# Rotary products and cached-score products of a hybrid decoder step put on VectorE in quarter steps, with half of the largest group's cached scores computed inside attention

## The chip, the cores and the metric

The kernel runs on one core of one Trainium2 chip, in one launch. The metric is the device time of that core in microseconds (us). The kernel before was timed three times: 1585.9, 1585.96 and 1590.62 us, a median of 1585.96 us. The profile is a further execution, with its own time of 1582.48 us.

## What is computed

The reference is one inference step of a two-layer decoder trunk for 512 prompt tokens and 8 x 8 sample tokens (576 tokens in all, 1024 channels). Layer 0 mixes with dilated attention, layer 1 with a state-space layer; each is followed by a gated feed-forward part. The change lies in the attention layer alone:

```python
qkv = (h @ w_qkv).reshape(B, T, 3, N_DIL, N_HEAD_SLOTS, HEAD_DIM)
q = rope(rmsnorm(qkv[:, :, 0], q_gain), pos)      # per head of 64
k = rope(rmsnorm(qkv[:, :, 1], k_gain), pos)
v = qkv[:, :, 2]
...
s = jnp.einsum('bqhd,bqkhd->bqhk', q_blk, kf) * (HEAD_DIM ** -0.5)
...
o = jnp.einsum('bqhk,bqkhd->bqhd', p, vf)         # for each of 3 groups
...
wts = jax.nn.softmax(jnp.stack(lses, axis=0), axis=0)
return jnp.einsum('gbqh,gbqhd->bqhd', wts, jnp.stack(outs, axis=0))
```

There are three groups (g = 0, 1, 2) with window and dilation (128, 1), (512, 4) and (2048, 16), each with 8 heads of 64. A sample token attends to cached keys and values (`cache_kv_w128`, `_w512`, `_w2048`) at those strides and to the 8 new tokens of its sequence. In group 2 the dilation is larger than the 8 new tokens, so each of the 8 queries of a sequence has its own 128 cached keys: 8 sequences x 8 queries x 128 keys x 512 channels are read. `rope` turns each head's two halves: x1*cos - x2*sin and x2*cos + x1*sin.

## The kernel before

**Projections** (`qkv_phase`, about 12 to 345 us of the profile). Nine chunks of 512 output channels are worked off in the order q, k, v of group 2, then of group 1, then of group 0. A chunk (`qkv_chunk`) has four steps of two 128-row weight tiles. In a step a weight block `raw` of 512 KB is loaded, split into a high part `whi` (ScalarE, L95) and a low part `wlo` (VectorE, L96: `raw - whi`), and multiplied with the split activations on TensorE (L320 to L326). `whi` and `wlo` have two buffers, so the split of a block waits for the matmuls of the block two before it, and TensorE waits for the split. Here and below line numbers are those of the kernel before.

After a q or k chunk its five token tiles are read out of PSUM (L476), squared and summed for the norm (L480, L481, then five small VectorE instructions L115 and L105 to L109), and a closure `finish(t)` per tile is put on the list `late`. `finish` rotates: VectorE multiplies with the cosines (L493, `t1`), GpSimd (POOL) multiplies the swapped halves with the sines (L495, `t2`) and adds (L496), VectorE scales with the norm (L498, `o`), TensorE transposes (L502) and ScalarE copies the result to `qT` or `kT`.

After each of the 36 steps a function `step()` runs: it pops `late` as the table `LATE` says, and starts the cached scores that the table `PLAN` names for that step. For groups 0 and 1 that is `score(gi, b)` for a sequence b, which transposes cached keys on TensorE. For group 2 it is `score2(b)`: four times it loads a tile `kc` of cached keys (512 KB) and a tile `qb` with the queries spread to all 128 partitions (512 KB, from the scratch `qscr`), multiplies the two (L404, by turns on VectorE and on POOL, into `kc`), and sums over each head's 64 channels with two reduces on VectorE (L406). The sums of all eight queries are then transposed, joined with the scores against the new keys, masked and stored in `Sall` (L408 to L417). All tiles `kc` and `qb` come from one pool `kst` of six buffers.

**Attention** (`attn_phase`, 345 to 477 us). Eight `decode(b)`, one per sequence, take the softmax of `Sall[b]`, transpose it (L628, L631), spread it into a padded tile (L633, L642), and multiply it with the cached values on TensorE (L655), whose seven tiles per sequence (six of 512 KB, one of 256 KB) come through the same six buffers of `kst`; then the new values (L658), a copy (L660) and a transpose back (L662). Four `prompt_pair(hp)`, one per pair of heads, run the prompt's scores, softmax (L598, L566 to L571 on VectorE, L568 on ScalarE), transposes (L602) and value products (L609, L615) in four rounds r each. The program's order is decode 2hp, pair hp, decode 2hp+1. After it, `wo_phase` needs all of `att`.

**Order.** The framework that builds the program (the tile scheduler) reorders instructions of an engine within what dependences and buffers allow; each engine then works strictly in the order written. DMAs of this part are issued by SyncE (SP), also in order: an issue that waits for a buffer holds up every one behind it.

Of the kernel before, what the change touches and what calls it, by code (L numbers as in the profile page):

```python
# [8 lines left out]
F32 = mybir.dt.float32  # L9
# [22 lines left out]
SCALE = HD ** -0.5  # L32
KST = 6
RV, RF = 0.0, 0.7
LATE = (2, 2, 1, 0)
PLAN = {11: (2,), 12: (2,), 14: (2,), 16: (2,), 20: (2,), 21: (2,), 22: (2, 1), 23: (2, 1), 24: (1,), 25: (1,), 26: (1,), 28: (1,), 30: (1,), 32: (1,), 34: (0, 0, 0), 35: (0, 0, 0)}


def dram(ap, off, dims):
    return bass.AP(tensor=ap.tensor, offset=ap.offset + off, ap=[list(d) for d in dims])  # L40
# [317 lines left out]
    return t  # L358


def qkv_phase(nc, tc, A, es, L):
    v, s, g, te = nc.vector, nc.scalar, nc.gpsimd, nc.tensor
    ident, rsqrt, pool = L["ident"], L["rsqrt"], L["pool"]
# [29 lines left out]
    wk = e3.enter_context(pool("wk1", bufs=2))  # L393
    qscr, vscr = L["qscr"], L["vscr"]

    def score2(b):
        q0 = T + b * 8
        P = dk.tile([128, 4, 4, 8], F32, name="ks")
        g.memset(P, 0.0)
        for c0 in range(0, 8, 2):  # L400
            kc = cache_tile(nc, A, kst, "kc", 2, b, c0, 2, 0)
            qb = kst.tile([128, 2, 512], F32, name="kc")
            nc.sync.dma_start(qb, dram(qscr, (b * 8 + c0) * 512, [[0, 128], [512, 2], [1, 512]]))
            (g if c0 % 4 else v).tensor_tensor(kc, kc, qb, OP.mult)  # L404
            for c in range(2):
                v.tensor_reduce(P[:, :, 0:2, c0 + c], kc[:, c].rearrange("p (a h d) -> p a h d", a=4, h=2), AX.X, OP.add)  # L406
        Q = dk.tile([128, 5, 4, 32], F32, name="Qz")
        g.memset(Q[:, 0], 0.0)  # L408
        for h in range(2):
            hs = slice(h * 64, h * 64 + 64)  # L410
            g.tensor_copy(Q[hs, 0, :, h * 8:h * 8 + 8], qT[2][hs, :, q0:q0 + 8])
        Sd = psd.tile([128, 136], F32, name="Sd")
        te.transpose(Sd[:, 0:128], P.rearrange("p a b c -> p (a b c)"), ident)
        for hp in range(4):
            te.matmul(Sd[hp * 32:hp * 32 + 32, 128:136], Q[:, 0, hp, :], kT[2][:, hp, q0:q0 + 8], start=True, stop=True,
                      tile_position=(0, hp * 32), skip_group_check=True)
        v.tensor_tensor_reduce(Sall[:, b, 2, :], Sd, md[:, 2, :], 1.0, -3e38, OP.add, OP.max, mx3[:, b, 2:3])  # L417

    def score(gi, b):
        q0 = T + b * 8  # L420
# [32 lines left out]
    turn = [0]  # L453

    def step():
        for _ in range(LATE[turn[0] % 4]):
            if late:
                late.pop(0)()
        for gi in PLAN.get(turn[0], ()):
            if fill[gi]:  # L460
                b = fill[gi].pop(0)
                score2(b) if gi == 2 else score(gi, b)
        turn[0] += 1

    late = []

    def qk_chunk(gi, part):
        ps = qkv_chunk(nc, A, L, x, part, gi, step, 0.0, x.prep if gi == 2 and part == 0 else None)
        sh = wk.tile([128, 5, 8], F32, name="sh")
        v.memset(sh[64:128, 4], 1.0)  # L470
        at = []
        for t in range(5):
            pp = 128 if t < 4 else 64
            a = wk.tile([128, 512], F32, name="a", bufs=5)
            if t < 4:
                s.activation(a, ps[t], AF.Copy, scale=(x.rb if gi == 0 else x.rc)[:, t:t + 1])  # L476
# [3 lines left out]
            s.activation(sq[:pp].rearrange("p h d -> p (h d)"), a[:pp], AF.Square)  # L480
            v.tensor_reduce(sh[:pp, t], sq[:pp], AX.X, OP.add)  # L481
            at.append(a)
        rq = wk.tile([128, 5, 8], F32, name="rq")
        rsqrt(rq, sh, 1.0 / HD, wk, [128, 5, 8])

        def finish(t):
            pp = 128 if t < 4 else 64
            ti = 8 if t == 4 else (4 + t if gi == 0 else t)
            a = at[t]
            t1 = wk.tile([128, 8, 64], F32, name="t1")  # L490
            t2 = wk.tile([128, 8, 2, 32], F32, name="t2", bufs=1)
            a4 = a.rearrange("p (h t d) -> p h t d", h=8, t=2)
            v.tensor_tensor(t1[:pp], a[:pp].rearrange("p (h d) -> p h d", h=8), C[part][:pp, ti, None, :].to_broadcast([pp, 8, 64]), OP.mult)  # L493
            Sv = S[part][:, ti, :].rearrange("p (t d) -> p t d", t=2)
            g.tensor_tensor(t2[:pp], a4[:pp, :, ::-1, :], Sv[:pp, None].to_broadcast([pp, 8, 2, 32]), OP.mult)  # L495
            g.tensor_tensor(t1[:pp], t1[:pp], t2[:pp].rearrange("p h t d -> p h (t d)"), OP.add)  # L496
            o = wk.tile([128, 512], F32, name="o")
            v.tensor_tensor(o[:pp].rearrange("p (h d) -> p h d", h=8), t1[:pp], rq[:pp, t, :, None].to_broadcast([pp, 8, 64]), OP.mult)  # L498
            dst = (qT, kT)[part][gi]
            pt = ptp.tile([128, 4, 128], F32, name="pt")  # L500
            for hp in range(4):
                te.transpose(pt[:, hp, :pp], o[:pp, hp * 128:(hp + 1) * 128], ident[:pp, :pp])  # L502
            s.activation(dst[:, :, t * 128:t * 128 + pp], pt[:, :, :pp], AF.Copy)
# [4 lines left out]
            if part == 1 and t == 4:  # L508
                fill[gi] += range(NB)

        late.extend((lambda t=t: finish(t)) for t in range(5))

# [23 lines left out]
    for gi in (2, 1, 0):  # L536
        while fill[gi]:
            score2(fill[gi].pop(0)) if gi == 2 else score(gi, fill[gi].pop(0))
# [10 lines left out]
def attn_phase(nc, tc, A, es, L):  # L549
# [20 lines left out]
        v.reciprocal(rd, den)  # L570
        v.tensor_scalar(sm, sm, rd, None, op0=OP.mult)  # L571

    def prompt_pair(hp):
        O = pO.tile([128, 4, 4, 32], F32, name="O")
        P0 = [wk.tile([128, 2, 4, 4, 32], F32, name=f"P0_{h}", bufs=1) for h in range(2)]
        for r in range(4):
            P12 = {}
            S2 = [pS.tile([128, 512], F32, name="S") for _ in range(2)]
            half = [slice(0, 64), slice(64, 128)]
            for b in range(4):  # L580
                for h in range(2):
                    hs = half[h]
                    q = qT[0][hs, hp, b * 128 + r:b * 128 + 128:4]
                    if b:
                        k = kT[0][hs, hp, (b - 1) * 128:(b + 1) * 128]
                        te.matmul(S2[h][b * 32:b * 32 + 32, 0:256], q, k, start=True, stop=True, tile_position=(h * 64, b * 32))
                    else:
                        k = kT[0][hs, hp, 0:128]
                        te.matmul(S2[h][0:32, 0:256].rearrange("p (a c) -> p a c", a=2), q, k[:, None, :].to_broadcast([64, 2, 128]), start=True, stop=True)
            for gi in (1, 2):  # L590
                sl = slice(r * 128, r * 128 + 128)
                for h in range(2):
                    te.matmul(S2[h][:, (gi + 1) * 128:(gi + 2) * 128], qT[gi][half[h], hp, sl], kT[gi][half[h], hp, sl], start=True, stop=True)
            for h in range(2):
                S = S2[h]
                sm = wk.tile([128, 512], F32, name="sm", bufs=3)
                mx = wk.tile([128, 1], F32, name="mx")
                v.tensor_tensor_reduce(sm, S, mp[:, r, :], 1.0, -3e38, OP.add, OP.max, mx)  # L598
                expnorm(sm, mx)
                pt = pP.tile([128, 4, 128], F32, name="pt")  # L600
                for c in range(4):
                    te.transpose(pt[:, c, :], sm[:, c * 128:(c + 1) * 128], ident)  # L602
                s.activation(P0[h][:, :, :, r, :], pt[:, 0:2, :].rearrange("p a (b i) -> p a b i", b=4), AF.Copy)
                p12 = wk.tile([128, 2, 128], F32, name="P12", bufs=3)
                v.tensor_copy(p12, pt[:, 2:4, :])
                P12[h] = p12
            for gi in (1, 2):
                for h in range(2):
                    te.matmul(O[h * 64:h * 64 + 64, r], vt[gi][:, r, (2 * hp + h) * 64:(2 * hp + h + 1) * 64], P12[h][:, gi - 1, :], start=gi == 1 and r == 0, stop=False, skip_group_check=True)  # L609
# [9 lines left out]
    def decode(b):  # L619
# [44 lines left out]
        for h in range(2):  # L664
            hs = slice(h * 64, h * 64 + 64)
            v.tensor_copy(att[hs, :, q0:q0 + 8], ot[hs, :, h * 8:h * 8 + 8])

    for hp in range(4):
        decode(2 * hp)
        prompt_pair(hp)  # L670
        decode(2 * hp + 1)


# [618 lines left out]
```

## Time and profile before

| | |
|---|---|
| median of three runs | 1585.96 us |
| the profiled execution's own time | 1582.48 us |
| its span, first to last instruction | 1580.7 us |
| TensorE (PE) busy | 1519.8 us, 96% |
| VectorE (DVE) busy | 917.6 us, 58% |
| ScalarE (ACT) busy | 527.0 us, 33% |
| GpSimd (POOL) busy | 433.4 us, 27% |
| mean granted TensorE clock | 0.992 |

The 1.8 us between span and own time lie outside the instructions. Times in the profile are us from the span's start. A row of the groups of instructions reads: line, engine, operation, tile written <- tiles read, shape, count | busy us, mean ns of one | idle time before them and what ended it. A row of the stages reads: start:end, width, then for each engine its busy us and (count), then the granted TensorE clock (1.00 is full), the share in which the 16 DMA engines were busy, and the GB/s they moved. A row of the timeline reads: start, duration, engine, line, operation, names, shape, count and, in brackets, the engine's idle time just before and what ended it. Each value product of a decode (L655) shows as two records, so that its 52 make 104.

### The profile page before, as it was taken

How to read it: one execution, taken by the hardware profiler on the slowest of the kernel's cores; microseconds unless marked ns; L12 is line 12 of the kernel's file. 1: busy time of each engine (PE TensorE's matmuls, PEld its weight loads, DVE VectorE, ACT ScalarE, POOL GpSimd, SP SyncE). 2: the span in 40 equal slices, each digit the busy share in tenths (PEclk: the TensorE clock that was granted, in tenths of full speed). 3: DMA queues.
4: the chain of work that ended last, by engine and by line, in shares of the span. 5: the costliest groups of instructions: out<-in, count | busy, mean ns of one | idle time of the engine just before them, and what ended most of it. 6: DMA issues, size and time to landing. Idle time of an engine off the chain costs nothing. (4 is left out here: it accounts for less than half of the span.)

```text
span 1580.7 us, 28939 instructions
## 1 busy us (share of the span) xinstructions
PE 1519.8 (96%) x12010; PEld 1425.8 (90%) x12010; DVE 917.6 (58%) x1557; ACT 527.0 (33%) x790; POOL 433.4 (27%) x407
## 2 busy tenths in 40 slices
PE   7989899979989999999999999999999999999998
PEld 6979777756669999999999999999999999999998
DVE  4787987445546785378878756775353333333332
ACT  5524334444434322123212244343242212221222
POOL 2464865440002101944524521021011001100100
PEclk9999999999998999999999999999999999999999
DMA  7398796484675555588767774875555555433212
GB/s 226 99 319 306 267 353 225 136 289 159 235 267 161 186 187 193 186 276 309 249 230 239 239 267 149 268 221 191 192 186 187 203 206 211 144 135 102 81 61 80
DMA packets 193843, 324.82 MB, mean 205 GB/s; under 512 B 40112, under 2 KB 137520, under 8 KB 192176
## 3 DMA queue, kind: packets, MB, share of 16 engines
q1 hardware_dynamic: 184256, 304.95, 56.5%
q10 hardware_dynamic: 9456, 18.03, 3.2%
q8 instruction: 94, 1.54, 0.4%
q14 instruction: 37, 0.30, 0.1%
HBM read 290.40 MB, written 119.83 MB: 260 GB/s over the span
## 5 line engine op out<-in xcount | busy, mean ns | idle before, releaser
L96 DVE TENSOR_TENSOR wlo<-raw,whi 128x1024 fp32r<-128x1024 f32 x200 | 256.2, 1282 | 265.1 <-ACT whi L95 261.6
L95 ACT ACTIVATE whi<-raw 128x1024 fp32r<-128x1024 f32 x200 | 208.2, 1042 | 522.3 <-PE acc L102 396.2
L102 PE MATMUL acc<-xgl,whi 128*128 128x288 f32 x1760 | 378.6, 296 | 1.0 <-DVE xgl L168 1.0
L102 PE MATMUL acc<-xgh,wlo 128*128 128x288 f32 x1760 | 377.6, 296 | 0.0
L102 PE MATMUL acc<-xgh,whi 128*128 128x288 f32 x1760 | 377.1, 296 | 0.1
L102 PEld LDWEIGHTS acc<-xgl,whi 128*128 128x128 f32 x1760 | 282.7, 188 | 2.6 <-DVE xgl L168 1.3
L102 PEld LDWEIGHTS acc<-xgh,wlo 128*128 128x128 f32 x1760 | 282.8, 188 | 0.6 <-issue 0.2
L102 PEld LDWEIGHTS acc<-xgh,whi 128*128 128x128 f32 x1760 | 281.7, 188 | 0.5 <-DVE gt L728 0.3
L730 POOL TENSOR_TENSOR gt<-gt,rstd 128x576 f32<-128x576 f32 x44 | 77.2, 1756 | 433.2 <-ACT gt L729 433.1
L102 PE MATMUL acc<-hh,whi 128*128 128x288 f32 x704 | 151.4, 296 | 0.0
L102 PE MATMUL acc<-hh,wlo 128*128 128x288 f32 x704 | 151.3, 295 | 0.0
L102 PE MATMUL acc<-hl,whi 128*128 128x288 f32 x704 | 151.1, 295 | 0.0
L321 PE MATMUL acc<-wlo,xh 128*128 128x512 f32 x288 | 118.7, 414 | 9.6 <-DVE wlo L96 9.6
L320 PE MATMUL acc<-whi,xh 128*128 128x512 f32 x288 | 111.5, 414 | 3.9 <-ACT a L522 3.7
L322 PE MATMUL acc<-whi,xl 128*128 128x512 f32 x288 | 113.7, 403 | 0.0
L102 PEld LDWEIGHTS acc<-hh,wlo 128*128 128x128 f32 x704 | 113.2, 188 | 0.2 <-issue 0.2
L102 PEld LDWEIGHTS acc<-hl,whi 128*128 128x128 f32 x704 | 113.0, 188 | 0.2 <-issue 0.2
L102 PEld LDWEIGHTS acc<-hh,whi 128*128 128x128 f32 x704 | 113.1, 188 | 0.0
L188 POOL TENSOR_TENSOR ssum<-ssum,sq 128x576 f32<-128x576 f32 x21 | 35.5, 1690 | 271.8 <-ACT sq L187 271.8
L321 PEld LDWEIGHTS acc<-wlo,xh 128*128 128x128 f32 x288 | 77.9, 270 | 16.1 <-DVE wlo L96 11.8
L320 PEld LDWEIGHTS acc<-whi,xh 128*128 128x128 f32 x288 | 75.5, 272 | 11.4 <-ACT a L522 4.9
L322 PEld LDWEIGHTS acc<-whi,xl 128*128 128x128 f32 x288 | 77.0, 271 | 4.2
(346 smaller groups left out, 2102.1 us busy)
## 6 DMA issues: line engine op xcount, KB each, us to landing
o_kv_s<-cache_kv_w SPq DMA_DIRECT2D x64, 1020.0 KB
kc<-cache_kv_w SPq DMA_DIRECT2D x96, 512.0 KB
raw<-ffn_w_gate SPq DMA_DIRECT2D x44, 512.0 KB
raw<-ffn_w_up SPq DMA_DIRECT2D x44, 512.0 KB
raw<-ffn_w_down SPq DMA_DIRECT2D x40, 512.0 KB
raw<-w_qkv SPq DMA_DIRECT2D x36, 512.0 KB
kc<-qscr SPq DMA_DIRECT2D x32, 512.0 KB
o_kv_s<-cache_kv_w SPq DMA_DIRECT2D x16, 1008.0 KB
```

What stands on the lines that cost most here:

```text
L95: s.activation(hi, raw, AF.Copy)
L96: v.tensor_tensor(lo, raw, hi.bitcast(F32), OP.subtract)
L102: te.matmul(ps[:, c, :HN], w, x[:, c * HN:(c + 1) * HN], start=first and i == 0, stop=last and i == 2)
L188: g.tensor_tensor(self.ss, self.ss, sq, OP.add)
L320: te.matmul(ps[t], ah, wh[:, k2, :], start=k == 0, stop=False)
L321: te.matmul(ps[t], ah, wl[:, k2, :], start=False, stop=False)
L322: te.matmul(ps[t], al, wh[:, k2, :], start=False, stop=k == KT - 1)
L730: g.tensor_tensor(t, t, nin.r, OP.mult)
```

## The change

Four things change. First, the sine product and the addition of the rotation (L495, L496) go from POOL to VectorE. Second, the products of `score2` are cut into four parts per sequence, each with one product and two reduces, so that the table names a part and not a sequence; in the projections all of them run on VectorE. Third, only the first four sequences (`EARLY = 4`) are done in the projections; the 16 parts of the other four are called in `prompt_pair`, two at the start of each round r, with the product on POOL, so that they stand in the first two pairs. Fourth, `LATE` and `PLAN` have new numbers. Sums over the heads stay on VectorE everywhere. The arithmetic and the work of TensorE are the same in total.

```diff
-LATE = (2, 2, 1, 0)
-PLAN = {11: (2,), 12: (2,), 14: (2,), 16: (2,), 20: (2,), ...
+EARLY = 4
+LATE, LAST = (2, 1, 1, 1), (2, 2, 1, 0)
+PLAN = {9: (2,), 11: (2,), 12: (2,), 13: (2,), 14: (2,), 15: (2,), ...
...
+def products(nc, A, L, eng, P, b, part):
+    kst, c0 = L["kst"], 2 * part
+    kc = cache_tile(nc, A, kst, "kc", 2, b, c0, 2, 0)
+    qb = kst.tile([128, 2, 512], F32, name="kc")
+    nc.sync.dma_start(qb, dram(L["qscr"], (b * 8 + c0) * 512, [[0, 128], [512, 2], [1, 512]]))
+    eng.tensor_tensor(kc, kc, qb, OP.mult)
+    for c in range(2):
+        nc.vector.tensor_reduce(P[:, :, 0:2, c0 + c], kc[:, c].rearrange("p (a h d) -> p a h d", a=4, h=2), AX.X, OP.add)
+
+def close2(nc, L, dk, psp, nm, P, b):
...
+    Sd = psp.tile([128, 136], F32, name=nm)
+    nc.tensor.transpose(Sd[:, 0:128], P.rearrange("p a b c -> p (a b c)"), L["ident"])
+    for hp in range(4):
+        nc.tensor.matmul(Sd[hp * 32:hp * 32 + 32, 128:136], Q[:, hp, :], kT[:, hp, q0:q0 + 8], start=True, stop=True,
+                         tile_position=(0, hp * 32), skip_group_check=True)
+    nc.vector.tensor_tensor_reduce(L["Sall"][:, b, 2, :], Sd, L["md"][:, 2, :], 1.0, -3e38, OP.add, OP.max, L["mx3"][:, b, 2:3])
...
-    def score2(b):
...
-            (g if c0 % 4 else v).tensor_tensor(kc, kc, qb, OP.mult)
...
+    def score2(b, part):
+        if part == 0:
+            prods[b] = dk.tile([128, 4, 4, 8], F32, name="P2", bufs=1)
+            g.memset(prods[b], 0.0)
+        products(nc, A, L, v, prods[b], b, part)
+        if part == 3:
+            close2(nc, L, dk, psd, "Sd", prods.pop(b), b)
...
-            g.tensor_tensor(t2[:pp], a4[:pp, :, ::-1, :], Sv[:pp, None].to_broadcast([pp, 8, 2, 32]), OP.mult)
-            g.tensor_tensor(t1[:pp], t1[:pp], t2[:pp].rearrange("p h t d -> p h (t d)"), OP.add)
+            v.tensor_tensor(t2[:pp], a4[:pp, :, ::-1, :], Sv[:pp, None].to_broadcast([pp, 8, 2, 32]), OP.mult)
+            v.tensor_tensor(t1[:pp], t1[:pp], t2[:pp].rearrange("p h t d -> p h (t d)"), OP.add)
...
-    def prompt_pair(hp):
+    def prompt_pair(hp, fill):
...
         for r in range(4):
+            for _ in range(2):
+                fill()
...
+    rest = [(b, p) for b in range(EARLY, NB) for p in range(4)]
+    def score2():
+        if not rest:
+            return
+        b, part = rest.pop(0)
...
+        products(nc, A, L, g, prods[b], b, part)
+        if part == 3:
+            close2(nc, L, dk, pD, "Sd", prods.pop(b), b)
...
-        prompt_pair(hp)
+        prompt_pair(hp, score2)
```

Below, line numbers are of the kernel in question: in the changed kernel the split is L98, the rotation L507 to L512, the product L368, its reduces L370, the closing L381 to L385, the decode's value product L672 and its transposes L645 and L679.

VectorE in the projections, while the group-2 queries are being rotated (`C` and `S` are the cosine and sine tables, `t` the two products, `rq` the norms). Before, ahead of a split:

```order
L498 TENSOR_TENSOR o<-t_537,rq 128x512
L498 TENSOR_TENSOR o<-t_550,rq 128x512
L493 TENSOR_TENSOR t_597<-a,C_150 128x512
L493 TENSOR_TENSOR t_610<-a,C_150 128x512
L96 TENSOR_TENSOR wlo<-raw,whi 128x1024
```

Now:

```order
L98 TENSOR_TENSOR wlo<-raw,whi 128x1024
L507 TENSOR_TENSOR t_597<-a,C_150 128x512
L507 TENSOR_TENSOR t_644<-a,C_150 128x512
L510 TENSOR_TENSOR t_597<-t_597,t_598 128x512
L509 TENSOR_TENSOR t_645<-a,S_152 128x512
L510 TENSOR_TENSOR t_644<-t_644,t_645 128x512
L512 TENSOR_TENSOR o<-t_597,rq 128x512
L509 TENSOR_TENSOR t_692<-a,S_152 64x512
L512 TENSOR_TENSOR o<-t_644,rq 128x512
L98 TENSOR_TENSOR wlo<-raw,whi 128x1024
```

A tile's rotation is now four VectorE instructions instead of two, so that eight stand between these two splits, and none of them waits for POOL any more.

SyncE's queue at the start of attention. `kc<-cache_kv_w` of 128x512 is the first value tile of a decode, the six of 128x2x512 behind it are its others; before, the tiles of decode 1 follow those of decode 0 directly:

```order
L357 DMA kc<-cache_kv_w 128x512
L357 DMA kc<-cache_kv_w 128x2x512 x6
L357 DMA kc<-cache_kv_w 128x512
L357 DMA kc<-cache_kv_w 128x2x512 x5
L645 DMA vn<-vscr 8x512 x3
```

Now the keys and queries (`kc<-qscr`) of eight parts stand between them:

```order
L359 DMA kc<-cache_kv_w 128x2x512 x7
L367 DMA kc<-qscr 128x1024
L359 DMA kc<-cache_kv_w 128x2x512
L367 DMA kc<-qscr 128x1024
...
L359 DMA kc<-cache_kv_w 128x2x512
L367 DMA kc<-qscr 128x1024
L359 DMA kc<-cache_kv_w 128x512
L359 DMA kc<-cache_kv_w 128x2x512 x6
L359 DMA kc<-cache_kv_w 128x512
```

The seven in the first row are the six of decode 0 and the first part's keys; decode 1 begins at the row of 128x512 after the eighth `qscr`. Decode 2 follows it, then eight more parts, then decode 3.

TensorE at the end of attention, from the last value products of the last pair (L615, now L632) to the first matmul of `wo_phase` (`ath`). Before:

```order
L615 MATMUL O<-P_1_4787,vt_2826 64x4x32
L655 MATMUL Sd<-kc,Pz_3331 32x128 x48
L658 MATMUL Sd<-vn,pn 32x128 x4
L662 MATMUL Sd<-ident,os 128x128
L102 MATMUL acc_5181<-ath,whi 128x288 x2
```

Now:

```order
L632 MATMUL O<-P_1_4787,vt_2513 64x4x32
L672 MATMUL Sd<-kc,Pz_3166 32x128 x8
...
L645 MATMUL Sd<-ident,Sall 128x128 x3
...
L672 MATMUL Sd<-kc,Pz_3167 32x128 x48
...
L672 MATMUL Sd<-kc,Pz_3166 32x128 x48
...
L672 MATMUL Sd<-kc,Pz_3167 32x128 x48
L675 MATMUL Sd<-vn,pn 32x128 x4
L679 MATMUL Sd<-ident,os 128x128
L104 MATMUL acc_5181<-ath,whi 128x288 x2
```

Before, one decode (the eighth) stands behind the last pair. Now the end of the fifth and the whole of the sixth, seventh and eighth stand there, with nothing of a pair between them.

More of the change, by code (lines that the diff above doesn't have):

```diff
@@ L394, in qkv_phase @@
     qscr, vscr = L["qscr"], L["vscr"]
-    def score2(b):
[L397 to L417, printed above, removed]
+    prods = {}
+    def score2(b, part):
[5 more added lines that the diff above has]
+            close2(nc, L, dk, psd, "Sd", prods.pop(b), b)
     def score(gi, b):
@@ L455, in step @@
     def step():
-        for _ in range(LATE[turn[0] % 4]):
+        for _ in range((LATE if turn[0] < 32 else LAST)[turn[0] % 4]):
             if late:
@@ L460, in step @@
             if fill[gi]:
[L461 to L462 removed]
+                x_ = fill[gi].pop(0)
+                score2(*x_) if gi == 2 else score(gi, x_)
         turn[0] += 1
@@ L507, in finish @@
                 nc.sync.dma_start(qscr, o[:64])
-            if part == 1 and t == 4:
-                fill[gi] += range(NB)
+            if t == 4 and part == (gi < 2):
+                fill[gi] += range(NB) if gi < 2 else [(b, p) for b in range(EARLY) for p in range(4)]
         late.extend((lambda t=t: finish(t)) for t in range(5))
@@ L535, in qkv_phase @@
     v_chunk(0, wk, vt)
-    for gi in (2, 1, 0):
+    assert not fill[2]
+    for gi in (1, 0):
         while fill[gi]:
-            score2(fill[gi].pop(0)) if gi == 2 else score(gi, fill[gi].pop(0))
+            score(gi, fill[gi].pop(0))
     e3.close()
```

13 lines of the change are left out of this document (12 added, 1 removed).

## The prediction

> **What bounds the kernel now.** I read the stages first: PE's idle time in each is its width less PE's busy time.
>
> ```profile
> 12.00:320.00 308.00, 289.15 (x1563) 250.53 (x1563) 223.87 (x306) 129.91 (x199) 173.78 (x169) 0.99 0.70 240
> 320.00:345.00 25.00, 17.61 (x288) 13.01 (x294) 10.34 (x37) 13.69 (x26) 13.31 (x30) 1.00 0.79 263
> 345.00:360.00 15.00, 12.49 (x170) 6.99 (x154) 4.85 (x17) 3.38 (x9) 0.00 (x0) 0.77 1.04 381
> 360.00:380.00 20.00, 20.00 (x184) 12.43 (x184) 14.51 (x64) 9.79 (x28) 0.00 (x0) 1.00 0.09 34
> 380.00:468.00 88.00, 83.80 (x1248) 57.24 (x1248) 47.04 (x203) 35.66 (x98) 0.00 (x0) 1.00 0.75 259
> 468.00:477.00 9.00, 4.53 (x102) 3.10 (x92) 0.81 (x3) 2.27 (x4) 0.00 (x0) 0.75 0.47 136
> 477.00:1580.70 1103.70, 1088.74 (x8473) 1079.63 (x8472) 612.36 (x922) 327.08 (x421) 245.75 (x203) 1.00 0.56 191
> ```
>
> PE bounds everything; its work does not change, so only its idle time can. That is 18.9 us in the nine chunks (12 to 320), 7.4 us behind the last chunk, 11.2 us in attention (2.5 + 0 + 4.2 + 4.5). From 477 on nothing moves, and I cost that part at nothing. PE's own waits in the chunks say what can go:
>
> ```profile
> PE acc L321 <- DVE wlo L96: 9.6, 5, 4.8
> PE acc L320 <- ACT a L522: 3.7, 3, 3.0
> PE pt L276 <- ACT xq L271: 2.5, 1, 2.5
> PE pt L502 <- DVE o L498: 1.6, 2, 1.2
> ```
>
> The longest of them, in the timeline of PE, VectorE and POOL:
>
> ```profile
> 97.45 0.82 PE L321 MATMUL acc<-wlo,xh 128*128 128x512 f32 x1 [4.77 <-DVE wlo L96]
> ...
> 93.11 0.96 DVE L106 TENSOR_TENSOR sq<-rq 128x40 f32<-128x40 f32 x1
> 94.00 3.40 DVE L96 TENSOR_TENSOR wlo<-raw,whi 128x1024 fp32r<-128x1024 f32 x1
> ...
> 93.98 2.34 POOL L404 TENSOR_TENSOR kc<-kc 128x1024 f32<-128x1024 f32 x1
> 96.27 2.26 POOL L495 TENSOR_TENSOR t<-a,S 128x512 f32<-128x512 f32 x1
> ...
> 72.57 1.21 DVE L96 TENSOR_TENSOR wlo<-raw,whi 128x1024 fp32r<-128x1024 f32 x1
> ```
>
> And the stage row of the 3.4 us behind that wait, the clock in the third column from its end:
>
> ```profile
> 97.00:100.40 3.40, 2.95 (x7) 2.41 (x8) 3.37 (x3) 0.00 (x0) 3.40 (x2) 0.50 0.55 164
> ```
>
> The same split takes 1.21 us elsewhere and 3.40 us here: it ends about a microsecond after POOL's product. [...] PE pays twice, since its granted clock is 0.50 in the 3.4 us after the stall (1.7 us lost).
>
> **The rotations.** The groups of VectorE and POOL up to 345 us:
>
> ```profile
> L495 POOL TENSOR_TENSOR t<-a,S 128x512 f32<-128x512 f32 (+1 forms) x30 | 53.4, 1779 | 13.6 <-ACT a L476 12.0
> L496 POOL TENSOR_TENSOR t<-t,t 128x512 f32<-128x512 f32 (+1 forms) x30 | 52.7, 1755 | 50.0 <-DVE t L493 36.8 <-ACT t L480 11.5 <-ACT qT L503 0.7
> L404 POOL TENSOR_TENSOR kc<-kc 128x1024 f32<-128x1024 f32 x16 | 41.1, 2570 | 10.2 <-DMA kc<-qscr 9.8
> ...
> L96 DVE TENSOR_TENSOR wlo<-raw,whi 128x1024 fp32r<-128x1024 f32 x38 | 55.0, 1450 | 27.9 <-ACT whi L95 27.7
> L406 DVE TENSOR_REDUCE ks<-kc 128x8 f32<-128x512 f32 x64 | 40.4, 674 | 0.3
> L106 DVE TENSOR_TENSOR sq<-rq 128x40 f32<-128x40 f32 x6 | 7.0, 1171 | 0.2
> ...
> 70.27 0.69 DVE L498 TENSOR_TENSOR o<-t,rq 128x512 f32<-128x512 f32 x1 [1.19 <-POOL t L496]
> ```
>
> POOL loses 106 us. VectorE gains 60 instructions; the nearest row is the free 0.69 us (a reversed operand could make it dearer, POOL's 1.78 us is the far bound): 41 us. It loses 32 of the 64 reduces, 32 x 0.674 = 22 us; its 16 products stay 16. It also loses the waits for POOL: on the splits alone 38 x (1.450 - 1.21) = 9 us, on the small norm step 6 x about 1 us. So VectorE stays near its 224 us of 308, but in pieces that no POOL instruction stretches, and spread: a sequence's scores put 2 x 1.21 + 8 x 0.674 = 7.8 us into one step before (a product has the split's 128x1024 shape), a part puts 1.21 + 2 x 0.674 = 2.6 us, and a step lasts about 8.6 us (308 in 36). Hence wlo's 9.6 us, o's 1.6 us and one clock drop of 1.7 us should go: 12.9, taken as **-13 us**. The ACT waits I leave standing. Bounds: -6 if half the queueing stays, -20 if all of 18.9 - 2.5 and two drops go.
>
> [...]
>
> **The closings.** Four transposes with their small matmuls move from one stage to the other. PE does them either way: nothing, their waits being counted below.
>
> **DMAs in attention.** Sixteen parts, two tiles each, join SP's queue between the decodes' value tiles:
>
> ```profile
> kc<-qscr SPq DMA_DIRECT2D x32, 512.0 KB
> ...
> DMA packets 16856, 30.41 MB, mean 230 GB/s; under 512 B 3200, under 2 KB 3264, under 8 KB 16708
> ...
> xT<-x_scr SPq DMA_DIRECT2D x1, 2304.0 KB
> ```
>
> Decode 0's last products and decode 1's first stand here on PE:
>
> ```profile
> 356.52 0.64 PE L655 MATMUL Sd<-kc,Pz 128*32 128x128 f32 x16
> ...
> 381.62 0.43 PE L655 MATMUL Sd<-kc,pa 128*32 128x128 f32 x8
> ```
>
> That is 16 x 2 x 0.524 = 16.8 MB on top of 30.4 MB (345 to 477), 47 MB. The full rate is that of the stage 345 to 360, 381 GB/s at a share of 1.04: 124 of 132 us. So the engines suffice on average, and the idle 360 to 380 takes 7.6 MB of the first eight parts' 8.4. [...]
>
> In the chunks SP's queue is rid of the same 16.8 MB; PE names no DMA among its waits there, so that is worth nothing.
>
> But order and buffers cost. VectorE's reduces now stand in its queue among the softmax steps: where one waits for POOL's product, the softmax behind it waits, and with it PE's transposes. Eight parts at 381 GB/s take 22 us; with three parts in six buffers, each held for its two transfers (2.8 us), the product (2.57 us) and VectorE's turn (1.35 us and a wait), 22 to 27 us. They start while decode 0 frees its buffers (its last products are the row at 356.52), say at 355, so the eighth part is reduced at 380 to 387, counted in times of the kernel before. The first pair ends where decode 1 begins now (381.62), and with one closing PE is there at about 383: a wait of 0 to 4 us. Decode 1's tiles follow, 3.4 MB, 9 us, partly beside the last parts: there by 389 to 394. PE's new order puts a round of the second pair ahead of decode 1. A round is about 6 us (345 to 468 less seven decodes at 4.5, in 16 rounds), so PE comes at 389: 0 to 5 us. The second eight parts cost the like of the first wait, 0 to 4. Together 0 to 13, middle **+6 us**.
>
> **The end of attention.** One decode stands behind the last pair now:
>
> ```profile
> 464.10 0.55 PE L628 MATMUL Sd<-ident,Sall 128*128 128x128 f32 x3
> ...
> 465.13 0.43 PE L655 MATMUL Sd<-kc,pa 128*32 128x128 f32 x8 [0.37 <-ACT pa L633]
> ...
> 467.59 2.39 PE L655 MATMUL Sd<-kc,Pz 128*32 128x128 f32 x80
> 472.66 1.08 PE L655 MATMUL Sd<-kc,Pz 128*32 128x128 f32 x16 [2.68 <-DMA kc<-cache_kv_w]
> 473.67 0.65 PE L658 MATMUL Sd<-vn,pn 24*32 24x128 f32 x8
> 474.78 0.47 PE L662 MATMUL Sd<-ident,os 128*128 128x128 f32 x1 [0.46 <-ACT os L660]
> 476.59 1.81 PE L102 MATMUL acc<-ath,whi 128*128 128x288 f32 x6 [1.33 <-ACT ath L682]
> ```
>
> Its 9.0 us (467.59 to 476.59) become those of three decodes and the fifth's rest. Alone, a decode needs 1.0 us from transposes to first product, 3.5 of products, 1.6 to its last transpose: 6.1 us. With six buffers the seventh and eighth can't be loaded ahead; 3.4 MB at 381 GB/s make 8.9 us each. So 2.1 (rest of the fifth decode) + 6.1 + 8.9 + 8.9 + 1.3 = 27.3 us against 9.0, +18.3. The pairs are shorter by the PE work that left them: for a decode 0.55 + 0.43 + 2.39 and, for the three last rows at full clock, about half of their 2.2, so 4.5 us, twice, and 1.4 of the fifth: +7.9. xT's 2.4 MB now stand ahead of the sixth decode's tiles (6 us, partly idle time): **+9 us**. Bounds: +2.5 with all tiles there (6.1 instead of 8.9, twice), +14 with all of xT.
>
> **The lock in attention.** POOL is idle there now (0.00 above). Sixteen products x 2.57 = 41 us will meet VectorE's softmax:
>
> ```profile
> L571 DVE TENSOR_SCALAR sm<-sm,rd 128x512 f32<-128x512 f32 x32 | 15.5, 485 | 0.7
> L566 DVE TENSOR_SCALAR nm<-mx 128x1 f32<-128x1 f32 x39 | 5.2, 145 | 0.2
> ...
> 98.62 2.27 DVE L108 TENSOR_SCALAR sq<-sq 128x40 f32<-128x40 f32 x1
> ```
>
> No row shows these beside POOL; the nearest is L108, also a tensor-scalar step, 2.27 us beside POOL's product. Some 16 of the 32 scalings and as many of the small steps fall among products; a third meeting one and losing about 1 us makes 10 us of VectorE time. VectorE is busy 14.5 of 20 us in the first pair, and the 16 reduces there add 11 us in some 35: it comes near full. I take **+4 us** on PE, 0 to 14.
>
> **The sum.** -13 + 0 + 6 + 9 + 4 = +6 us. On the profiled execution's 1582.5 us that is 1588.5. The median of the runs, 1586.0, lies 3.5 us higher, and the forecast stands on it: **1592 us**.
>
> **The rivals.**
> (a) *The loads hide (faster).* If decode 1 and the closings find their data, the waits are 0 and the end costs its lower +2.5; with -14 in the chunks and no lock cost: -12, 1574 us. For it: the idle 360 to 380. Against: three decodes in a row with nothing to cover them, which is order, not chance. It decides where decode 1's last tile lands: by 389 it wins.
> (b) *Even.* -16 in the chunks (one ACT wait goes too) with attention at +16: 1586 us.
> (c) *VectorE becomes attention's bound.* Softmax, reduces and lock exceed the pairs' time, and every late reduce holds the six buffers: waits 13, lock 14, end 9, chunks -13, +23: 1609 us. It decides when the scalings lose over 1 us each time they meet a product. [...]
> (d) *No gain in the chunks.* VectorE is as full as before and splits queue as long: -3 with attention's +19: 1602 us. It comes about if the 60 new instructions cost near POOL's 1.78 us: 107 us, and VectorE stands at 224 + 107 - 22 - 15 = 294 of 308. Against: the free 0.69 us of the same shape.
>
> Chances: forecast 0.37, (a) 0.20, (b) 0.25, (c) 0.11, (d) 0.07. About 0.3% (4.8 us) is what a measurement of this kernel can tell from none: faster by more 0.20, within 0.25, slower 0.55. The range reaches from (a) to (c): 1574 to 1610.
>
> **What would show it.** In the chunks: splits at 1.21 us throughout, wlo's wait near zero, no 0.50 clock near 97. In attention: scalings over 1 us beside POOL's product, waits of PE for the closing's sums and for decode 1's tiles, and three decodes of 6 to 9 us behind the last pair, the clock below 1.00 there. I am wrong if attention lasts no longer than now, or if wlo's waits stay.

## The result, and the profile after

The changed kernel takes 1597.5 us (median of 20 runs, 1589.2 to 1602.5), the kernel before beside it 1585.6 us: a ratio of 1.0071, 95% interval 1.0059 to 1.0083. It is slower by 11 us. The profiled execution spans 1595.0 us, 14.3 more than the 1580.7 of before. The profiled execution of before has a mean granted clock of 0.992, where the 86 executions of it beside the experiments below have 0.968 to 0.992, with a median of 0.986.

The stages of the changed kernel (the chunks, the tail behind them, the four pairs, the decodes behind the last pair, the rest; columns as in the stages above):

```profile
12.00:296.00 284.00, 278.15 (x1475) 246.74 (x1477) 199.08 (x323) 128.70 (x198) 30.16 (x71) 0.99 0.58 200
296.00:326.00 30.00, 22.53 (x365) 16.90 (x372) 7.59 (x38) 15.13 (x27) 9.83 (x37) 0.89 0.86 300
326.00:368.00 42.00, 40.50 (x375) 25.39 (x375) 34.93 (x99) 14.76 (x40) 20.25 (x12) 0.76 0.75 262
368.00:397.00 29.00, 28.17 (x417) 19.24 (x417) 16.19 (x72) 11.58 (x35) 0.87 (x5) 1.00 0.75 252
397.00:437.00 40.00, 36.11 (x228) 22.11 (x224) 27.78 (x84) 11.49 (x32) 19.85 (x12) 0.57 0.71 242
437.00:457.00 20.00, 17.86 (x313) 12.83 (x313) 11.01 (x46) 8.49 (x25) 0.00 (x0) 1.00 0.90 331
457.00:491.30 34.30, 21.82 (x377) 13.28 (x377) 3.80 (x29) 3.44 (x13) 0.00 (x0) 0.75 0.87 297
491.30:1595.00 1103.70, 1088.04 (x8473) 1078.91 (x8473) 607.94 (x922) 327.86 (x421) 247.18 (x203) 1.00 0.56 191
```

From wo's first matmul on, both kernels take 1103.7 us. In the chunks PE's idle time is 284.00 - 278.15 = 5.9 us, where it was 18.9. The first round starts at 325.9 and no longer at 344.7 (-18.8), yet wo starts at 491.3 and no longer at 476.6 (+14.7): attention takes 165.4 us for 131.9, 33.5 more.

PE's waits in the chunks, all of them:

```profile
PE acc L322 <- ACT a L536: 3.0, 1, 3.0
PE pt L278 <- ACT xq L273: 2.5, 1, 2.5
PE acc L322 <- ACT xh L280: 0.3, 1, 0.3
```

wlo's 9.6 us are gone. VectorE's groups in the chunks, the split and one of the rotation's two new steps:

```profile
L98 DVE TENSOR_TENSOR wlo<-raw,whi 128x1024 fp32r<-128x1024 f32 x36 | 44.5, 1239 | 30.4 <-ACT whi L97 29.9 <-DMA o_kv_p<-a 0.2
...
L509 DVE TENSOR_TENSOR t<-a,S 128x512 f32<-128x512 f32 x24 | 16.3, 680 | 3.8 <-ACT a L490 3.6
```

The split averages 1.24 us, where it was 1.45, and the reversed operand costs nothing (0.68 us). VectorE's groups in the pairs, from 326 to 457:

```profile
L615 DVE CUSTOM_DVE_ANT_0 sm<-S,mp 128x512 f32<-128x512 f32 x32 | 21.7, 685 | 15.3 <-PE pt L619 10.8 <-PE S L610 4.3
L586 DVE TENSOR_SCALAR sm<-sm,rd 128x512 f32<-128x512 f32 x32 | 21.3, 666 | 0.4
L370 DVE TENSOR_REDUCE P<-kc 128x8 f32<-128x512 f32 x32 | 20.2, 675 | 3.4 <-POOL kc L368 3.3
L622 DVE COPY P<-pt 128x256 f32<-128x256 f32 x32 | 13.2, 416 | 5.4 <-ACT P L620 5.4
L586 DVE TENSOR_SCALAR Sall<-Sall,rd 128x408 f32<-128x408 f32 x7 | 6.4, 915 | 0.1
```

The scalings average 0.67 us for 0.485. The reduces wait only 3.3 us for POOL. What VectorE waits for is PE (15 us ahead of the first softmax step). PE's longest waits between the chunks' end and wo:

```profile
PE Sd L672 <- DMA kc<-cache_kv_w: 10.2, 13, 1.7
PE pt L455 <- DMA kc<-cache_kv_w: 5.3, 1, 5.3
PE Sd L679 <- ACT os L677: 2.1, 4, 0.7
PE S L606 <- DVE mx L615: 1.8, 2, 1.6
PE O L626 <- DVE nm L581: 1.8, 1, 1.8
```

Its idle time there is 28.3 us by the stages above (30.00 - 22.53 in the tail, 20.8 in attention), where before had 18.6 (7.4 and 11.2). So waits make 10 of the 33 us. The rest is in the clock column. First the first pair of before, then windows of the changed kernel, cut where its granted clock changes:

```profile
345.00:382.90 37.90, 35.39 (x425) 22.14 (x413) 19.59 (x81) 14.31 (x38) 0.00 (x0) 0.91 0.46 169
```

```profile
345.88:366.36 20.48, 19.74 (x121) 12.97 (x120) 19.16 (x55) 6.51 (x18) 12.13 (x9) 0.50 0.62 213
366.36:400.49 34.13, 32.02 (x453) 21.41 (x449) 19.00 (x79) 13.57 (x38) 3.17 (x5) 1.00 0.79 273
400.49:434.62 34.13, 31.52 (x180) 19.06 (x180) 25.04 (x71) 9.71 (x26) 17.56 (x11) 0.50 0.72 241
434.62:457.00 22.38, 20.25 (x339) 14.63 (x339) 12.56 (x55) 9.92 (x27) 0.00 (x0) 1.00 0.82 301
```

54.6 us of the pairs pass at half clock (0.09 x 2 x 37.9 = 6.8 before). They lie where POOL is busy: the first eight parts run in the first pair, the second eight in the third and not, as I had it, in the second. PE is recorded busy there, 31.5 of 34.1 us, but its own work takes longer. The counts, 180 and 453, don't show by how much, since 234 of the 453 belong to decodes; the same four transposes do, ahead of the first drop and behind the second:

```profile
343.92 0.63 PE L619 MATMUL pt<-ident,sm 128*128 128x128 f32 x4 [0.76 <-DVE sm L586]
401.61 1.12 PE L619 MATMUL pt<-ident,sm 128*128 128x128 f32 x4
```

### The profile page after: what moved, and what is told of

It is laid out like the page before. It is cut to its first block, busy times and chain, and to the rows that moved or that the text cites. A ratio compares the mean times of both kernels' runs of the same rounds, so it can differ in the third digit from the quotient of the medians.

```text
span 1595.0 us, 28876 instructions
## 1 busy us (share of the span) xinstructions
PE 1537.3 (96%) x12010; PEld 1438.7 (90%) x12010; DVE 912.4 (57%) x1617; ACT 527.1 (33%) x790; POOL 329.8 (21%) x347
## 5 line engine op out<-in xcount | busy, mean ns | idle before, releaser
L98 DVE TENSOR_TENSOR wlo<-raw,whi 128x1024 fp32r<-128x1024 f32 x200 | 247.3, 1237 | 275.7 <-ACT whi L97 271.9
## 6 DMA issues: line engine op xcount, KB each, us to landing
kc<-cache_kv_w SPq DMA_DIRECT2D x96, 512.0 KB
raw<-ffn_w_gate SPq DMA_DIRECT2D x44, 512.0 KB
raw<-ffn_w_up SPq DMA_DIRECT2D x44, 512.0 KB
raw<-ffn_w_down SPq DMA_DIRECT2D x40, 512.0 KB
raw<-w_qkv SPq DMA_DIRECT2D x36, 512.0 KB
kc<-qscr SPq DMA_DIRECT2D x32, 512.0 KB
```

Source lines behind the costliest of these rows:

```text
L98: v.tensor_tensor(lo, raw, hi.bitcast(F32), OP.subtract)
```

## The experiments

The theory at first: the chunks gain because the rotations and products no longer lock VectorE (stretch its steps, as the split's 3.40 us for 1.21 beside POOL's product), and attention gives it back at the pace of the parts. The rivals: the lock, the loads and their order, and a VectorE that is too full in the projections with all the scores. Ratios are to the kernel before beside the same runs, with 95% intervals; 0.01 is 15.9 us. "Attention" is from the first round to wo's first matmul in the profiled execution.

**The rotations alone.**

```
-            g.tensor_tensor(t2[:pp], a4[:pp, :, ::-1, :], ...
-            g.tensor_tensor(t1[:pp], t1[:pp], t2[:pp]...
+            v.tensor_tensor(t2[:pp], a4[:pp, :, ::-1, :], ...
+            v.tensor_tensor(t1[:pp], t1[:pp], t2[:pp]...
```

> The kernel before, with the rotation's two POOL steps on VectorE and nothing else. Theory (the chunks gain by the rotation's and the products' locks going, and attention gives it back): most of the gain in the chunks stands here and attention stays as before, so about 1578 us, 1574 to 1582. Rival (the gain in the chunks comes from the half of the scores that left them, since VectorE is too full with all of them): within 3 us of the kernel before, 1583 to 1589.

Ratio 0.9968 (0.9933 to 1.0003), not separable from no change; the median, 1586.8 us, lies in the rival's range. PE's waits in the chunks:

```profile
PE acc L320 <- ACT a L522: 9.1, 3, 3.9
PE pt L276 <- ACT xq L271: 3.6, 1, 3.6
...
PE acc L321 <- DVE wlo L96: 0.8, 2, 0.6
```

wlo's waits went as predicted, but the wait for the eviction `a` grew from 3.7 to 9.1 us, and the first round starts at 345.0, as before.

**All eight sequences in the projections.**

```
-EARLY = 4
+EARLY = 8
-PLAN = {9: (2,), 11: (2,), ...
+PLAN = {9: (2,), 10: (2, 2), 11: (2,), ...
```

> The changed kernel with all eight sequences' parts in the projections (32 parts on VectorE, one in nearly every step from the ninth), none in attention. Theory: the chunks keep a gain of 8 to 16 us and attention is as before: 1570 to 1579 us. Rival (VectorE is too full with 32 parts and the rotations, the moved half is what made the gain): 1584 to 1595 us, with wlo's waits back.

Ratio 1.0000 (0.9959 to 1.0041), median 1594.3 us: the rival's time, but not by wlo's waits. The first round starts at 349.9. PE waits 0.8 us for wlo, and elsewhere for the fuller VectorE:

```profile
PE acc L326 <- DVE a L336: 6.1, 1, 6.1
PE pt L515 <- DVE o L511: 5.8, 1, 5.8
```

So the rotations don't earn the projections' gain by themselves, nor with the products in quarters: the stalls move to the next wait until 16 parts leave VectorE as well. The parts moved out with the rotations left on POOL weren't run. This kernel also shows the price of the clock. Of its ten executions four took 1576.8 to 1580.4 us at a granted clock of 0.983 to 0.987, five took 1593.8 to 1598.4 at 0.972 to 0.975, and one 1604.6 at 0.966. The means of the four and the five are 17.7 us apart; 0.012 of clock over 1590 us is 19 us of full-speed time.

**Attention's products on VectorE.**

```
-        products(nc, A, L, g, prods[b], b, part)
+        products(nc, A, L, v, prods[b], b, part)
```

> The changed kernel with attention's 16 products on VectorE instead of POOL. Rival (the lock between POOL's products and VectorE's softmax steps is what attention loses by): the scalings fall back to 0.48 us, attention's pairs get shorter by 10 us or more, 1580 to 1588 us. Theory (the pairs go at the pace of the parts, load, product, reduces in VectorE's order, and TensorE falls to half its clock): the half clock stays, VectorE gets 19 us of products into the two pairs and the time stays within 5 us of the changed kernel's 1597, 1592 to 1602.

Ratio 1.0070 (1.0041 to 1.0099), the changed kernel's. Its pairs, and the scalings in them:

```profile
325.80:466.90 141.10, 123.18 (x1439) 81.06 (x1437) 99.55 (x322) 48.23 (x129) 2.91 (x12) 0.82 0.82 272
```

```profile
L586 DVE TENSOR_SCALAR sm<-sm,rd 128x512 f32<-128x512 f32 x32 | 15.5, 483 | 0.5
```

The scalings are back at 0.48 us and nothing is won: the loss needs no lock.

**One part a round.**

```
-            for _ in range(2):
-                fill()
+            fill()
```

> The changed kernel with one part a round instead of two, so that the 16 parts lie in all four pairs. Theory (pace of the parts, half clock, and three decodes behind the last pair): TensorE waits less in the first two pairs, the decodes lie one by one between the pairs as before, the end behind the last pair falls from 35 us to 15 to 25: 1580 to 1588 us. Rival (lock: the same 16 products meet the same softmax steps): within 4 us of the changed kernel, 1593 to 1601. Second rival (only the DMA order at the end counts): the last pair's parts hold the last sequence's scores up and the end is no shorter, 1595 or more.

Ratio 1.0158 (1.0104 to 1.0211). I was wrong. Behind the last pair the end did fall, from 34.0 to 18.5 us (493.5 to 512.0), but the last pair grew to 63.6, and there the second rival has the reason: the last sequences' closings stand in it now, and PE waits for them. From 430 us on:

```profile
PE Sd L381 <- DVE P L370: 16.2, 2, 13.9
PE Sd L671 <- DMA kc<-cache_kv_w: 8.5, 6, 5.2
PE pt L618 <- DVE sm L586: 8.0, 1, 8.0
```

**Denser rounds.** After these, the half clock was the suspect. This kernel adds matmuls that compute nothing which is used (`wz` holds bf16 copies of some queries):

```
...
+            for h in range(2):
+                for _ in range(2):
+                    te.matmul(S2[h], wz[:, 0:128], wz, start=True, stop=True)
```

> The changed kernel with 64 more matmuls in attention's rounds, 128x128 by 128x512 in bf16, two into each score tile ahead of its own products, which write over them. They compute nothing that is used: they only make TensorE's work denser, for some 14 us at full clock if nothing hides them. New theory (the loss is the half clock: a thin stretch in the rounds drops it, and the rounds' own small products don't lift it, so it stays until the pair's end): the half clock in attention's pairs falls from 55 us to under 20, and the time stays at the changed kernel's or falls, 1585 to 1598 us. Rival (the half clock only follows from waits on loads and parts that are there anyway): half clock as before, and the matmuls come on top, 1600 to 1612.

Its pairs, its added matmuls, and four of them in a row:

```profile
326.10:460.00 133.90, 125.68 (x1498) 77.02 (x1497) 85.15 (x306) 48.62 (x129) 40.65 (x28) 0.96 0.79 274
```

```profile
L601 PE MATMUL S<-wz x64: 376/379/634, 325.1 to 442.2; 128*128 128x512 bf16 x64
```

```profile
325.14 1.02 PE L601 MATMUL S<-wz 128*128 128x512 bf16 x4
```

The half clock in the pairs falls from 55 to 10 us (0.04 x 2 x 133.9) in this execution. It is the shortest of the ten (1595.3 us, the median is 1606.8), with a granted clock of 0.984; all ten have 0.968 to 0.984, mean 0.978, and the changed kernel's twenty 0.970 to 0.978, mean 0.974. So denser work of PE goes with a somewhat higher clock, on average by far less than this profile shows. Attention takes 163.7 us for 165.4, with 64 matmuls more. Overlapped they take some (1.02 - 0.38) / 3 = 0.21 us each, 14 us in all: what the clock gives back, they take. The ratio is 1.0088 (1.0052 to 1.0124), and the median lies in the rival's range.

**A stall in the rounds of the kernel before**, twice. The first put four additions on tiles of their own ahead of the third pair's softmax:

```
+                for _ in range(4):
+                    v.tensor_tensor(jk[0], jk[0], jk[1], OP.add)
```

> The kernel before with four additions of 128x1024 on VectorE (on zeros that nothing reads, 1.21 us each) ahead of the softmax of the third pair's first round: one stall of TensorE of some 4 us, and nothing else. New theory (half clock stays to the pair's end): 20 to 35 us at half clock follow, and the time grows by 12 to 22 us, to 1598 to 1608. Rival (a stall costs its length and one window of half clock, as in the chunks): 3 to 7 us, to 1589 to 1595.

It tested nothing: the additions have no input from the round, and the trace has them at 331 to 337 us, ahead of attention. Ratio 1.0001 (0.9966 to 1.0036). The second ties them to the round:

```
+                for _ in range(12 if (hp, r, h) == (2, 0, 0) else 0):
+                    v.tensor_tensor(sm, S, mp[:, r, :], OP.add)
```

> The kernel before with twelve additions of the third pair's first score tile and the mask, 128x512, each into the tile that the softmax step behind them overwrites, so that they can't move: some 7 us of VectorE ahead of one softmax, and nothing else. Theory (a thin stretch in the rounds drops the clock, and the rounds' small products don't lift it): 20 us or more at half clock follow and the time grows by more than the stall, by 13 to 22 us against the kernel before, to 1600 to 1612. Rival (a stall costs what it lasts and two windows): 4 to 9 us, 1592 to 1598.

Ratio 1.0027 (0.9994 to 1.0061), not separable from no change. The first pair, the third, and the step of 3.41 us in which PE has least to do around the additions:

```profile
348.00:391.00 43.00, 42.33 (x345) 25.49 (x347) 19.64 (x81) 13.29 (x37) 0.00 (x0) 0.66 0.39 144
421.70:457.20 35.50, 33.11 (x466) 21.79 (x462) 25.00 (x100) 16.25 (x45) 0.00 (x0) 1.00 0.52 182
422.38:425.79 3.41, 2.47 (x57) 1.45 (x46) 2.81 (x9) 0.70 (x3) 0.00 (x0) 1.00 1.00 324
```

With 8.3 us of additions (414.7 to 425.7) the third pair takes 35.5 us for 30.7, and the clock stays at 1.00. My theory that one thin stretch is enough falls for a stretch of this depth, 2.47 of 3.41 us; PE has a decode's products to do meanwhile, and its longest wait there is 0.7 us, so a deeper stall wasn't made. The rival's price isn't shown either: the first pair of this execution, to which nothing was added, passes 29 us at half clock (0.34 x 2 x 43.0).

**What of the parts costs: loads, reduces, products.** These three kernels leave out arithmetic that the last four sequences' scores need, and show only what it costs.

```
+    if not work:
+        return
     eng.tensor_tensor(kc, kc, qb, OP.mult)
...
-        products(nc, A, L, g, prods[b], b, part)
+        products(nc, A, L, g, prods[b], b, part, False)
```

> The changed kernel with attention's 16 parts only loaded: their 16 products on POOL and 32 reduces on VectorE are left out (the last four sequences' scores are those of zeros). If the reduces that wait for POOL's products in VectorE's order, or the lock, make the thin stretches: the third pair's half clock (34 us) goes, the first pair's may stay: 1575 to 1588 us. If the loads make them (order and bandwidth): within 5 us of the changed kernel, 1592 to 1602.

```
-    for c in range(2):
+    for c in range(2 if red else 0):
...
+        products(nc, A, L, g, prods[b], b, part, True, False)
```

> The changed kernel with attention's 16 parts loaded and multiplied on POOL, but their 32 reduces on VectorE left out (the last four sequences' scores are those of zeros). Theory (VectorE's 20 us of reduces between the softmax steps thin TensorE's work and make the half clock): near the kernel whose parts are only loaded, 1576 to 1584 us, no half clock in the pairs. Rival (POOL's products cost, by the lock or by holding two buffers 2.6 us longer): near the changed kernel, 1591 to 1600.

```
-    eng.tensor_tensor(kc, kc, qb, OP.mult)
+    if prod:
+        eng.tensor_tensor(kc, kc, qb, OP.mult)
...
+        products(nc, A, L, g, prods[b], b, part, False, True)
```

> The changed kernel with attention's 16 parts loaded and reduced on VectorE, but their 16 products on POOL left out (the last four sequences' scores are sums of keys alone). Theory (the reduces): near the changed kernel, 1590 to 1600 us, with 30 us or more at half clock in the pairs. Rival (the products): near the kernel whose parts are only loaded, 1576 to 1584.

The ratios are 0.9918 (0.9891 to 0.9946) for the loads alone, 0.9992 (0.9959 to 1.0026) with products and no reduces, 0.9949 (0.9918 to 0.9981) with reduces and no products; the medians are 1578.6, 1587.7 and 1581.7 us. The pairs of the three in this order, one window each:

```profile
328.70:428.10 99.40, 97.56 (x1190) 63.03 (x1187) 60.65 (x256) 46.62 (x123) 2.28 (x12) 1.00 0.86 309
```

```profile
327.90:434.20 106.30, 99.94 (x1170) 64.51 (x1171) 77.14 (x256) 46.68 (x123) 41.11 (x28) 0.98 0.81 282
```

```profile
325.60:437.00 111.40, 107.14 (x1340) 71.56 (x1344) 79.74 (x297) 47.84 (x126) 2.28 (x12) 0.94 0.88 316
```

Loads without arithmetic leave the pairs at full clock, and this kernel gains 13 us on the one before. Products alone add 0.0074, reduces alone 0.0031, both together 0.0153 (24 us). The excess over the sum, 0.0048, is no wider than these intervals, so it isn't shown. My theory (the reduces are the cost) is wrong as put: the time without them lies between the two answers, and the time without the products in the rival's range. But the products alone don't make the 24 us either. Half clock in the pairs, from these rows: 0, 4 and 13 us, and 55 with both. The 13 comes from the shortest of ten executions (1574.2 us); by the median granted clock of all ten, 0.982 each, products alone and reduces alone are alike, with 0.986 for the loads alone and 0.973 for both. The scalings beside POOL's products, without the reduces:

```profile
L587 DVE TENSOR_SCALAR sm<-sm,rd 128x512 f32<-128x512 f32 x32 | 27.8, 870 | 0.3
L587 DVE TENSOR_SCALAR Sall<-Sall,rd 128x408 f32<-128x408 f32 x7 | 8.3, 1196 | 0.0
```

**Buffers of their own for the parts.**

```
+    kpt = es.enter_context(pool("kpt", bufs=4))
-        products(nc, A, L, g, prods[b], b, part)
+        products(nc, A, L, g, prods[b], b, part, kpt)
```

> The changed kernel with four buffers of their own for attention's parts, so that the decodes' value tiles have the six alone. If the shared ring holds the fourth decode and the three at the end up: the 35 us behind the last pair become 20 to 28 and the time 1580 to 1590. If SP's order, the bandwidth and the half clock set the end: within 4 us of the changed kernel, 1593 to 1601.

Ratio 1.0082 (1.0041 to 1.0122): no gain, as the second answer had it. Behind the last pair (from 466.1) it still takes 41.7 us, in the longest of its ten executions; nothing here says that the six shared buffers hold the end up.

**The clock in the first pair.** The kernel with the rotations alone, and unused matmuls in its first pair:

```
...
+            if hp == 0:
+                for h in range(2):
+                    for _ in range(1):
+                        te.matmul(S2[h], wz[:, 0:128], wz, start=True, stop=True)
```

> The kernel before with the rotation's steps on VectorE, and eight of the unused bf16 matmuls in the first pair alone, one into each score tile (0.38 us each, 3 us). Theory: the 34 us at half clock that this kernel without them had in the first pair go, its times lie closer together (1579 to 1600 without), and the median is 1579 to 1584. Rival (one per tile is too little, or the half clock has another cause): the spread stays and the median is 1587 to 1592.

Ratio 1.0002 (0.9981 to 1.0023), median 1589.0 us: the rival's time. The first pair:

```profile
348.00:389.90 41.90, 38.30 (x478) 23.63 (x473) 22.43 (x91) 15.40 (x41) 0.00 (x0) 0.88 0.49 173
```

It has 10 us at half clock (0.12 x 2 x 41.9) where the rotations alone had 34, and the spread is narrower, as the theory had it (1585.8 to 1593.9, against 1579.0 to 1600.4). But the mean granted clock over all executions hardly moves (0.985 for 0.984), and no time is won. No version here that computes everything is shown to beat the kernel before.

## Why the prediction was right, step by step

The forecast was 1592 us, slower by 6; it came out slower by 11. The direction is right, and that the size came this near is partly luck, since the terms were off in opposite directions. By the profiled executions attention starts 18.8 us earlier (term -13), loads, order and closings cost 10.5 (terms +15), and the arithmetic costs 23 (term +4).

*The chunks, -13.* PE's idle time there fell by 13.0 us (18.9 to 5.9): right in size, with the split at 1.24 us and wlo's waits gone. The first round comes 18.8 us earlier; the other 5.8 are PE's recorded busy time ahead of it, which holds the four closings that now stand behind, and I can't divide it further. The reason was incomplete: I put the gain down to instructions that POOL no longer stretches. The rotations alone removed those waits (wlo's 9.6 us fell to 0.8), and PE waited for `a` instead (9.1 us). With the 16 parts' work off VectorE as well that wait is 3.0 us; which of the two halves would do without the other was tried for the rotations only.

*Rival (d)*, VectorE as full as before with splits that queue as long, is out: the new steps cost 0.68 us. Rivals (a) and (b) are excluded by the interval.

*DMA and order, +6, and the end, +9.* Together 15. With loads, order and closings but no arithmetic, attention takes 142.4 us (328.7 to 471.1) for 131.9: +10.5, and some of that is the closings. The waits I priced at +6 are not in the list of waits: PE names no closing, and of the loads 1.7 us in the pairs, 8.5 behind the last pair, and one of 5.3 in the tail, which I hadn't foreseen. The three decodes do stand uncovered, and longer than I said: 34.0 us where I had 27.3, at a clock of 0.75 and 297 GB/s.

*The lock, +4 (0 to 14).* This is the term that was mis-sized. Its own working holds: the scalings lost (21.3 - 15.5) + (6.4 - 7 x 0.43) = 9.2 us of VectorE time, where I had 10. But I gave 4 us to the path for everything that the arithmetic does, and it costs 23 (165.4 - 142.4) or, by the ratios, 24. The lock is not needed for it (products on VectorE: the same time). It is there, though: nine of the 32 scalings overlap a product of POOL and take 1.14 us on average, up to 2.57, where they take 0.48 without. The reduces show no such stretch: 17 of the 32 overlap a product of POOL and take 0.677 us on average, the other 15 take 0.673. Why the one step is stretched and the other isn't, no run shows. The prediction saw VectorE come near full in the first pair, but gave it no price of its own, and it left out the clock within the pairs.

VectorE's time in a round that carries parts, from the rows: the softmax takes 2 x (0.685 + 0.485 + 0.416 + 0.38 for the three small steps) = 3.9 us. Two parts add 4 x 0.675 = 2.7. The lock adds 9.2 / 8 = 1.1, without the reduces ((27.8 - 15.5) + (8.3 - 3.0)) / 8 = 2.2, and the products on VectorE 2 x 1.21 = 2.4. The prediction's estimate for PE is about 6 us a round.

| kernel | VectorE a round | half clock in the profiled pairs | median clock of all executions |
|---|---|---|---|
| loads alone | 3.9 us | 0 us | 0.986 |
| products alone | 6.1 us | 4 us | 0.982 |
| reduces alone | 6.6 us | 13 us | 0.982 |
| changed kernel | 7.7 us | 55 us | 0.973 |
| products on VectorE | 9.0 us | 51 us | 0.971 |

The median clock falls as VectorE's round grows past PE's. A reading that fits is that PE's work thins there, its clock halves, and PE is the slower one after all: so the profile shows a busy PE and hardly a wait. That the crossing is the cause is argued, not shown. Against it as the whole cause, the kernel with eight sequences in the projections has a median clock of 0.974 with no part in its rounds, and the products alone cost more time than the reduces alone (0.0074 for 0.0031, with intervals that overlap) at a shorter round. The size of the loss does fit the clock: half of 54.6 - 6.8 is 24 us, and by the medians, 0.973 for 0.986, it is 0.013 x 1590 = 21 us.

*Rival (c)* named VectorE as attention's bound and came nearest in mechanism, but its condition wasn't met: scalings that meet a product were to lose over 1 us each, and the nine lost 0.65 on average (1.14 less 0.485), three of them over 1.

*Open:* what exactly drops the clock. The kernels with only the rotations and with eight sequences in the projections had 34 us at half clock in the first pair with no part in it, and the stalled pair kept its clock. Rounds with almost no decode between them, first of the kernel with loads alone, then of the one with eight sequences in the projections:

```profile
338.65:369.37 30.72, 30.72 (x304) 19.95 (x297) 21.66 (x93) 15.75 (x43) 1.52 (x8) 1.00 0.84 307
357.23:391.36 34.13, 34.13 (x175) 20.08 (x171) 15.94 (x68) 10.92 (x30) 0.00 (x0) 0.50 0.04 13
```

PE is recorded busy throughout both, and VectorE less in the second than in the first. So rounds of the same kind were run through at either clock, and a VectorE that is too full isn't needed for the low one. What the parts' arithmetic does, by whatever step, is make such spells the rule: with it the changed kernel's twenty executions have clocks of 0.970 to 0.978, and with the loads alone the ten have 0.982 to 0.989.

## What to carry to other kernels

Before work is moved into a stage where two engines are near balance, add up each engine's time per round there with the moved work in it. Here the kernels with the longest VectorE rounds had the lowest clock, and most of the loss showed as a busy TensorE whose instructions took longer, not as a wait: so read the clock column beside the waits, and over several executions. And a wait removed is a gain only if the next one on the same engine isn't due at the same time: test each half of a change alone.

## What the runs showed of the hardware

The clock stayed low with PE busy for most of the time. In both profiled executions the granted clock changes in steps of 3.41 us: in the kernel before, the spells at 0.50 up to 483 us last 3.41, 3.41, 6.83 and 10.24 us. In the changed kernel it is 0.50 from 400.5 to 434.6, ten steps in a row, while PE is recorded busy for 31.5 of the 34.1 us, and PE's longest gap at their start is 1.8 us (the wait for nm above). The step ahead of the drop has PE busy for 2.13 of 3.41 us, so it wasn't idle there. In five of the ten steps PE is recorded busy throughout, and the clock came back only behind the tenth. Both long spells end some 2 us ahead of the end of their pair (366.4 and 434.6; the pairs' sums are evicted by 368.1 and 437.1). In the eight-sequence kernel, where PE is recorded busy for all of 34.1 us (the row above), it also came back behind the tenth. A round's small products at half clock, 13 to 22 in each of the first nine steps from 400.5 on, didn't bring it back there. The denser kernel, at a mean clock of 0.978 for 0.974, suggests that more products help, and doesn't show that they bring it back.

SyncE's queue held still for a buffer. In the kernel before it issues nothing from 359.8 to 382.1 us: its next issue (L357) waits 22.3 us for a decode's value products (L655), and from 360 to 380 the DMAs move 34 GB/s.
